# Two stacked transformer blocks in split fp32: the memory keys kept as high and low parts, and four raw weight buffers instead of six

## The chip, the cores and the metric

One Trainium2 chip, one core of it. The metric is the device time of one execution of the whole program, in microseconds; the kernel before took 2056.8 us (median of 3 runs, 2055.86 to 2057.23).

## The reference

Two transformer blocks on one sequence of 256 rows of width 1024, all in fp32. The first has four layers, each a mixer, a cross attention to a memory of 256 rows and a feed-forward part with a short convolution, with a layer norm behind each. The second has two layers with other mixers that attend to a second memory. What bears on the change is this:

```python
mem_k, mem_v = jnp.split(mem @ mem_w_kv, 2, axis=-1)      # once, for all four layers
...
def memory_cross_attention(x, mem_k, mem_v, w_q, w_o):    # 4 heads of 256
    q = (x @ w_q).reshape(bsz, s, X_HEADS, X_HEAD_DIM)
    sc = jnp.einsum('bshd,bmhd->bhsm', q, mem_k).astype(jnp.float32) * (X_HEAD_DIM ** -0.5)
    p = jax.nn.softmax(sc, axis=-1)
    o = jnp.einsum('bhsm,bmhd->bshd', p.astype(mem_v.dtype), mem_v).reshape(bsz, s, D_MODEL)
    return o @ w_o
...
for i in range(DEPTH):                                    # 4 layers
    y = mixer(x)                                          # window attention, recurrent, latent, window attention
    x = layer_norm(ALPHA * x + y, ln_g[i, 0], ln_b[i, 0])
    x = layer_norm(ALPHA * x + memory_cross_attention(x, mem_k, mem_v, x_w_q[i], x_w_o[i]), ...)
    x = layer_norm(ALPHA * x + conv_glu_ffn(x, ...), ...)
```

## The kernel before

The 256 rows are two tiles of 128 partitions (t = 0 and 1); the width 1024 is eight blocks of 128 (KD). X, the residual, stays in SBUF in row form. What a matmul needs in transposed form is transposed on TensorE (L262) and split into two fp32r parts: the high part is a cast on ACT, the low part a subtract on DVE (`split`, L163 and L164). Every large product of two fp32 operands is then three matmuls, high by high, high by low and low by high (`mm3`, L158 to L160).

Weights go through `wslot`. One slot is 128x1024 in fp32, 512 KB (384 KB and less in a few products): one DMA from SP's queue into a buffer of the pool `wraw` (L77), two casts of 512 columns on ACT into hi (L83), and two subtracts on DVE into lo (L86). The second subtract sets the raw buffer free. hi and lo come from a second pool of nine slots. There are 650 slots in one execution. The pools are rings: a DMA into a raw buffer waits for the subtract that read the slot which had the buffer before, and SP takes its DMAs strictly in order, so whatever stands behind a blocked one waits too. Among those are the DMAs of the layer norms' gains and biases (`gb`, 1 MB, one buffer, L404, which waits for the last L420 of the norm before).

The program is written as cooperative threads (a dense product, an attention lane, the transposes of a row tile), and the `run` loop emits them by a planned clock; after that each engine's instructions are put in order once more by a list scheduler. So a change of a pool's size also changes the order in which an engine gets its instructions. The engines run their queues in order.

The keys and values of the memory are made first, before any layer: `mem_kv_first` computes eight key blocks of 128x256 (slots 0 to 7, `mem_w_k`) and two value tiles of 128x1024 (slots 8 to 15, `mem_w_v`), and `evac` copies them from PSUM into `memkv`, in turn with ACT (L62) and DVE (L64). The constants (identity, rope tables, mask; L245 to L254) are loaded within it; the mask's staging buffer waits for the softplus of the recurrent layer's parameters on DVE (L197 to L207). Each of the four crosses then casts the whole key tile to its own kh on ACT (L630, four casts) and takes kl by four subtracts on POOL (L631). Beside these, POOL only does the power in a few one-column instructions (L396, L1082).

A layer norm (`layer_norm_post`) adds the PSUM banks to X (L412), takes statistics (L413, L415), the scale (L395 on DVE, L396 on POOL), and then X by L419 and L420, all on DVE but for L396; behind it PE transposes X (L262). In the second block `norm_first` takes the sum of squares on ACT (L1079), the scale on DVE and POOL (L1081, L1082), and the normed row on DVE (L1084).

Of the kernel before, what the change touches and what calls it, by code (L numbers as in the profile page):

```python
# [12 lines left out]
F32 = mybir.dt.float32  # L13
F32R = mybir.dt.float32r
AF = mybir.ActivationFunctionType
ALU = mybir.AluOpType
# [3 lines left out]
P = 128  # L20
NT = 2
D = 1024
KD = D // P
# [5 lines left out]

M_SWA1, M_CAUS1, M_CAUS0, M_END = 0, 256, 384, 512  # L30

CFG = dict(hm=(1, 1), pm=(2, 2), cut=2, raw=6, hl=9, tail=8, head=3, pin=())


@with_exitstack
def model_kernel(ctx: ExitStack, tc: tile.TileContext, A, out):
    nc = tc.nc
    V, S, G, T = nc.vector, nc.scalar, nc.gpsimd, nc.tensor

    const = ctx.enter_context(tc.tile_pool(name="const", bufs=1))  # L40
    wraw = ctx.enter_context(tc.tile_pool(name="wraw", bufs=CFG["raw"]))
    whl = ctx.enter_context(tc.tile_pool(name="whl", bufs=CFG["hl"]))
    act = ctx.enter_context(tc.tile_pool(name="act", bufs=1))
# [4 lines left out]
    def bank(tag="r"):  # L48
        return psum.tile([P, 512], F32, tag=tag, name="bank", bufs=4 if tag == "r" else 2)
# [4 lines left out]
    def phase(name):  # L54
        return tc.tile_pool(name=name, bufs=2, reuse_waits="tile")
# [3 lines left out]
    def evac(dst, src):  # L59
        count["ev"] += 1  # L60
        if count["ev"] % 2:
            S.copy(dst, src)  # L62
        else:
            V.tensor_copy(dst, src)  # L64

    ring = deque(maxlen=CFG["hl"])

# [3 lines left out]
    def wslot(src, pieces, held=idle):  # L71
        res, o = [], 0
        for m in pieces:
            assert len(ring) < CFG["hl"] or not ring[0]()
            ring.append(held)
            raw = wraw.tile([P, 1024], F32, tag="raw", name="raw")
            nc.sync.dma_start(raw[:, :m], src[:, o : o + m])  # L77
            hi = whl.tile([P, 1024], F32R, tag="hi", name="hi")
            lo = whl.tile([P, 1024], F32R, tag="lo", name="lo")
            step = -(-m // CFG["cut"])  # L80
            for a in range(0, m, step):
                c = slice(a, min(a + step, m))
                S.copy(hi[:, c], raw[:, c])  # L83
            for a in range(0, m, step):
                c = slice(a, min(a + step, m))
                V.tensor_tensor(lo[:, c], raw[:, c], hi[:, c], ALU.subtract)  # L86
            res.append((hi, lo))
            o += m
        return res
# [6 lines left out]
    def pe(ins):  # L96
        if pinned[0] in CFG["pin"]:
            tc.keep_in_program_order(ins)
# [16 lines left out]
    def after(*ths):  # L115
        def f():
            if all(t is None or t.done for t in ths):
                return max([t.end for t in ths if t is not None] + [0.0])
            return None

        return f
# [34 lines left out]
    def mm3(ps, ah, al, bh, bl, first, last):  # L156
        clk[0] += 3 * (ps.shape[-1] / 2.4 + 13.5)
        pe(T.matmul(ps, ah, bh, start=first, stop=False))  # L158
        pe(T.matmul(ps, ah, bl, start=False, stop=False))  # L159
        pe(T.matmul(ps, al, bh, start=False, stop=last))  # L160

    def split(hi, lo, src):
        S.copy(hi, src)  # L163
        V.tensor_tensor(lo, src, hi, ALU.subtract)  # L164
# [14 lines left out]
        return wide(tag + "h", F32R), wide(tag + "l", F32R)  # L179

    cur = {}
    memkv = act.tile([P, 4, D], F32, tag="mkv", name="memkv")

    readers = {"x": [], "o": []}
    rows_of = [None, None]
# [27 lines left out]
    head = []  # L213
    with phase("init") as ph:
# [7 lines left out]
        for h in range(4):  # L222
            if h == 1:
                head = wslot(A["mem_w_k"][0], [1024, 1024])
            c = slice(2 * h, 2 * h + 2)
# [4 lines left out]
    def load_x():  # L230
        nc.sync.dma_start(X, A["x"])
        with phase("initx") as ph:
            xT = fresh("x")
            for h in range(4):
                c = slice(2 * h, 2 * h + 2)
                stage = ph.tile([P, 2, NT * P], F32, tag="stage", name="stage")
                nc.sync.dma_start(stage, A["xT"][:, c])
                split(xT[0][:, c], xT[1][:, c], stage)
# [5 lines left out]
    def load_constants():  # L244
        nc.sync.dma_start(ident, A["c_ident"])  # L245
        S.copy(identr, ident)
        nc.sync.dma_start(rope, A["c_rope"])
        with phase("initm") as ph:
            mst = ph.tile([P, M_END], F32, tag="mst", name="mst")
            nc.sync.dma_start(mst, A["c_mask"])  # L250
            S.copy(maskh, mst)
            sst = ph.tile([P, 2, 12], F32, tag="sst", name="sst")
            nc.sync.dma_start(sst, A["c_sel"])
            S.copy(sel, sst)  # L254
# [11 lines left out]
    def transpose_split(blocks, dst, t):  # L266
        def put(i, n, ps):
            split(dst[0][:, i : i + n, tile_cols(t)], dst[1][:, i : i + n, tile_cols(t)], ps)

        transposed(blocks, put)  # L270
# [16 lines left out]
    def col_blocks(x, n=KD):  # L287
        return [x[:, i * P : (i + 1) * P] for i in range(n)]
# [80 lines left out]
    def load_rows(w, n, per):  # L369
        return Rows(w, n, per)  # L370
# [3 lines left out]
    def project_full(src, w, post):  # L374
        project(src, load_rows(w, D, 1), HALVES, post)
# [9 lines left out]
    def rows_ready():  # L385
        return [after(r) for r in rows_of]

    def by_block(w):
        for s in range(w.shape[0]):
            for hi, lo in wslot(w[s], [1024, 1024]):  # L390
                yield hi.rearrange("p (k c) -> p k c", c=P), lo.rearrange("p (k c) -> p k c", c=P)
# [207 lines left out]
    def fed(*ths):  # L599
        return lambda: 0.0 if all(t.fed for t in ths) else None  # L600
# [4 lines left out]
    def mem_kv_first():  # L605
        first = [[x.rearrange("p (k c) -> p k c", c=P) for x in b] for b in head]
        for c, (hi, lo) in enumerate(chain(first, by_block(A["mem_w_k"][1:]))):
            ps = bank()
            for k in range(KD):
                mm3(ps[:, :256], hi[:, k], lo[:, k], cur["o"][0][:, k], cur["o"][1][:, k], k == 0, k == KD - 1)  # L610
            evac(memkv[:, c // 4, (c % 4) * 256 : (c % 4 + 1) * 256], ps[:, :256])
            if c == 5:
                load_constants()

        def post(t, ps):
            for h in range(2):
                evac(memkv[:, 2 + t, h * 512 : (h + 1) * 512], ps[h])
            if t == 0:
                load_x()

        project_full(cur["o"], A["mem_w_v"], post)

    def cross(i, post):
        pinned[0] = "s"
        with phase(f"x{i}") as ph:
            kT = memkv[:, 0:2].rearrange("p a (c n) -> p (a c) n", n=256)
            kh = ph.tile([P, KD, 256], F32R, tag="kh", name="kh", bufs=1)
            kl = ph.tile([P, KD, 256], F32R, tag="kl", name="kl", bufs=1)
            for c in range(0, KD, 2):
                S.copy(kh[:, c : c + 2], kT[:, c : c + 2])  # L630
                G.tensor_tensor(kl[:, c : c + 2], kT[:, c : c + 2], kh[:, c : c + 2], ALU.subtract)  # L631

            tq, at = {}, []
            lane = Lane(1, 3, old_read)

            def qpost(t, ps):
                q = ph.tile([P, D], F32, tag="q", name="q", bufs=1)
                for h in range(2):
                    S.mul(q[:, h * 512 : (h + 1) * 512], ps[h], 1.0 / 16)
                soon = clk[0] + 1500  # L640
                yield lambda: soon if t == 0 or lane.recs[0].scored is not None else None
                qh = ph.tile([P, KD, P], F32R, tag="qh", name="qh", bufs=1)
                ql = ph.tile([P, KD, P], F32R, tag="ql", name="ql", bufs=1)
                transpose_split(col_blocks(q), (qh, ql), 0)
                tq[t] = qh, ql

            def score_of(t):
                def score(h):
                    qh, ql = tq[t]
                    return [  # L650
                        (l[:, k], r[:, k])
                        for k in range(2 * h, 2 * h + 2)
                        for l, r in ((qh, kh), (ql, kh), (qh, kl))
                    ]

                return score

            ws, ready = load_rows(A["x_w_q"][i], D, 1), rows_ready()
            q = [dense("x", ws, HALVES, t, qpost, need=ready[t], lag=1700) for t in range(NT)]
            for t in range(NT):  # L660
                at.append(attend(
                    lane, ph, t, 4, 256, 256, score_of(t), lambda h, kt: memkv[:, 2 + kt, h * 256 : (h + 1) * 256],
                    need=lambda h0: after(q[t]), hold=fed(q[t]), cost=720,
                ))
            out_proj(A["x_w_o"][i], post, *at)
            run(*at[0], *at[1])
# [778 lines left out]
```

## Time and profile before

| what | us |
|---|---|
| runs of the kernel before, median of 3 | 2056.8 (2055.86 to 2057.23) |
| profiled execution, its own time | 2056.11 |
| span of its trace | 2054.3 |
| TensorE (PE) busy | 2028.4 (99%) |
| VectorE (DVE) busy | 1603.8 (78%) |
| ScalarE (ACT) busy | 1214.3 (59%) |
| GpSimd (POOL) busy | 59.6 (3%) |
| granted TensorE clock, mean | 0.999 |

The busy time of an engine is a sum over the span; it tells nothing of which of its waits are on the path that sets the end. That is read from the waits: a row "A <- B" there says that an instruction of A sat idle until B had finished. A wait of SP's queue (SPq) for a buffer is what a prefetch looks like when it is far ahead. HBM was read at 173 GB/s over the span, 354.75 MB.

### The profile page before, as it was taken

What the parts mean: (1) busy time and instruction counts of PE and PEld (TensorE: products, weight loads), DVE (VectorE), ACT (ScalarE), POOL (GpSimd) and SP (SyncE); (2) the same over time, 40 slices, a digit from 0 to 9 for tenths busy, and PEclk for the clock granted to TensorE, in tenths of its full rate; (3) what the DMA queues carried; (4) which work ended last, traced back from release to release, by engine and by line L of the source; (5) the groups of instructions that cost most, each with busy time, mean ns of one, the idle gap of its engine ahead of it and who ended that gap; (6) DMA issues with size and microseconds to landing.
All of it is one profiled execution on the core that took longest, in us unless ns stands there. A gap on an engine that the chain in (4) does not pass through costs nothing.

```text
span 2054.3 us, 35609 instructions
## 1 busy us (share of the span) xinstructions
PE 2028.4 (99%) x13290; PEld 1832.5 (89%) x13290; DVE 1603.8 (78%) x3327; ACT 1214.3 (59%) x2642; POOL 59.6 (3%) x62
## 2 busy tenths in 40 slices
PE   8999999999999999999999999999999999999998
PEld 7788999897899988889997889998988999988997
DVE  6887878789777788697789878787668877778775
ACT  6655656496565556465556556565556665557563
POOL 0010000002000001000000100000000000000000
PEclk9999999999999999999999999999999999999999
DMA  8533655536455452455544447554346555445551
GB/s 300 208 134 134 226 188 182 180 112 242 153 197 186 154 183 103 175 201 195 187 149 164 145 145 254 195 182 151 121 142 235 202 180 170 126 145 202 188 185 52
DMA packets 101407, 358.12 MB, mean 174 GB/s; under 512 B 11889, under 2 KB 13553, under 8 KB 99313
## 3 DMA queue, kind: packets, MB, share of 16 engines
q1 hardware_dynamic: 101232, 355.84, 49.6%
q8 instruction: 104, 1.70, 0.3%
q14 instruction: 71, 0.57, 0.1%
HBM read 354.75 MB, written 1.05 MB: 173 GB/s over the span
## 4 chain that ended last, share of the span: by engine, by line
PE 91%; DVE 5%; ACT 2%; DMA 1%; issue 1%; POOL 0%; SPq 0%; POOLq 0%; DVEq 0%; ACTq 0%
PE bank L158 27%; PE bank L160 27%; PE bank L159 27%; PE bank L557 3%; PE bank L262 2%; DVE lo L86 2%; PE bank L488 1%; PE bank L529 1%; PE bank L483 1%; ACT hi L83 1%; PE bank L478 1%; ACT pr L508 0%; DMA row<-in_mem 0%; DVE nm L501 0%; PE bank L1037 0%
## 5 line engine op out<-in xcount | busy, mean ns | idle before, releaser
L83 ACT CAST hi<-raw 128x512 fp32r<-128x512 f32 (+3 forms) x1300 | 745.2, 607 | 438.9 <-PE bank L159 202.6
L86 DVE TENSOR_TENSOR lo<-raw,hi 128x512 fp32r<-128x512 f32 (+3 forms) x1300 | 840.9, 671 | 182.7 <-ACT hi L83 178.0
L158 PE MATMUL bank<-xh,hi 128*128 128x256 f32 (+1 forms) x1936 | 547.9, 283 | 0.6 <-ACT ti L803 0.6
L160 PE MATMUL bank<-xh,lo 128*128 128x256 f32 (+1 forms) x1936 | 547.6, 283 | 0.0
L159 PE MATMUL bank<-xl,hi 128*128 128x256 f32 (+1 forms) x1936 | 547.5, 283 | 0.0
L158 PEld LDWEIGHTS bank<-xh,hi 128*128 128x128 f32 x1936 | 371.3, 192 | 4.1 <-ACT ti L803 0.9
L159 PEld LDWEIGHTS bank<-xl,hi 128*128 128x128 f32 x1936 | 371.3, 192 | 2.7
L160 PEld LDWEIGHTS bank<-xh,lo 128*128 128x128 f32 x1936 | 371.3, 192 | 0.4
L977 DVE SCALAR_TENSOR_TENSOR c<-bank,cw,c 128x254 f32<-128x254 f32 (+1 forms) x528 | 238.7, 477 | 31.0 <-ACT c L973 30.6
L158 PE MATMUL bank<-hi,xh 128*128 128x512 f32 (+4 forms) x688 | 249.5, 363 | 0.0
L160 PE MATMUL bank<-hi,xl 128*128 128x512 f32 (+4 forms) x688 | 242.1, 353 | 0.5 <-DVE xl L164 0.5
L159 PE MATMUL bank<-lo,xh 128*128 128x512 f32 (+4 forms) x688 | 241.8, 352 | 0.0
L158 PE MATMUL bank<-hi,gh 128*128 128x512 f32 x528 | 208.7, 395 | 0.2 <-ACT gh L163 0.2
L159 PE MATMUL bank<-lo,gh 128*128 128x512 f32 x528 | 206.5, 391 | 0.0
L160 PE MATMUL bank<-hi,gl 128*128 128x512 f32 x528 | 205.5, 390 | 0.0
L158 PE MATMUL bank<-hi,oh 128*128 128x512 f32 (+1 forms) x392 | 157.6, 404 | 0.0
L159 PE MATMUL bank<-lo,oh 128*128 128x512 f32 (+1 forms) x392 | 152.2, 389 | 0.5 <-DVE lo L86 0.5
L160 PE MATMUL bank<-hi,ol 128*128 128x512 f32 (+1 forms) x392 | 152.3, 389 | 0.0
L158 PEld LDWEIGHTS bank<-hi,xh 128*128 128x128 f32 x688 | 129.7, 188 | 16.2 <-issue 2.9
L160 PEld LDWEIGHTS bank<-hi,xl 128*128 128x128 f32 x688 | 129.4, 188 | 14.4 <-DVE xl L164 0.7
L159 PEld LDWEIGHTS bank<-lo,xh 128*128 128x128 f32 x688 | 129.8, 189 | 11.9
L973 ACT ACTIVATE c<-bank,cw 128x256 f32<-128x256 f32 x264 | 133.5, 558 | 0.2 <-PE bank L160 0.2
(270 smaller groups left out, 2495.1 us busy)
## 6 DMA issues: line engine op xcount, KB each, us to landing
raw<-in_f_w_up SPq DMA_DIRECT2D x176, 512.0 KB, 3.6
raw<-in_f_w_down SPq DMA_DIRECT2D x88, 512.0 KB, 3.5
raw<-in_m_w_up SPq DMA_DIRECT2D x88, 512.0 KB, 4.0
raw<-in_m_w_down SPq DMA_DIRECT2D x44, 512.0 KB, 3.6
raw<-in_m_w_qkv SPq DMA_DIRECT2D x48, 384.0 KB, 3.6
raw<-in_x_w_q SPq DMA_DIRECT2D x32, 512.0 KB, 3.5
raw<-in_x_w_o SPq DMA_DIRECT2D x32, 512.0 KB, 5.4
raw<-in_a_w_qkv SPq DMA_DIRECT2D x24, 512.0 KB, 6.0
```

Of the source, the lines that this page charges most:

```text
L83: S.copy(hi[:, c], raw[:, c])
L86: V.tensor_tensor(lo[:, c], raw[:, c], hi[:, c], ALU.subtract)
L158: pe(T.matmul(ps, ah, bh, start=first, stop=False))
L159: pe(T.matmul(ps, ah, bl, start=False, stop=False))
L160: pe(T.matmul(ps, al, bh, start=False, stop=last))
L262: pe(T.transpose(ps[:w, j * P : (j + 1) * P], b, ident))
L478: pe(T.matmul(banks[b], l, r, start=(j == 0), stop=False))
L483: pe(T.matmul(banks[b][:, i], l, r, start=(j == 0), stop=(j == len(pairs) - 1)))
L488: pe(T.matmul(banks[b][:, i], *pairs[j], start=False, stop=(j == count_ - 1 and i == g - 1)))
L557: pe(T.matmul(po[i * w : (i + 1) * w, tile_cols(c - c0)], value(h0 + h, kt)[:, off : off + w], pT[h, kt], start=(kt == 0), stop=(kt == nk ...
L973: S.activation(c[:, h], ps[:, h], AF.Identity, scale=cw[:, 2, b : b + 1], bias=cw[:, 3, b : b + 1])
L977: V.scalar_tensor_tensor(c[:, h, s:], ps[:, h, : 256 - s], cw[:, 2 - s, b : b + 1], c[:, h, s:], ALU.mult, ALU.add)
```

## The change

The memory keys are no longer kept in fp32 and split anew in each cross. `mem_kv_first` writes them by `split`, so a key block costs one ACT cast from PSUM and one DVE subtract that reads PSUM and the high part; the tile `memk` holds both parts and takes the place of `memkv`, 16 KB in each partition. The values get a tile of their own, `memv`, 8 KB. The crosses read `memk` directly, and kh, kl and their casts and subtracts (L630, L631) are gone. For the 8 KB, the raw weight ring gets four buffers instead of six. Lines behind L181 move down by one and, behind the removed ones, up by five (L404 becomes L405, L1084 becomes L1079).

```diff
-CFG = dict(hm=(1, 1), pm=(2, 2), cut=2, raw=6, hl=9, tail=8, head=3, pin=())
+CFG = dict(hm=(1, 1), pm=(2, 2), cut=2, raw=4, hl=9, tail=8, head=3, pin=())
...
-    memkv = act.tile([P, 4, D], F32, tag="mkv", name="memkv")
+    memk = act.tile([P, 2, KD, NT * P], F32R, tag="mkv", name="memk")
+    memv = act.tile([P, NT, D], F32, tag="mv", name="memv")
...
-            evac(memkv[:, c // 4, (c % 4) * 256 : (c % 4 + 1) * 256], ps[:, :256])
+            split(memk[:, 0, c], memk[:, 1, c], ps[:, :256])
...
-                evac(memkv[:, 2 + t, h * 512 : (h + 1) * 512], ps[h])
+                evac(memv[:, t, h * 512 : (h + 1) * 512], ps[h])
...
-            kT = memkv[:, 0:2].rearrange("p a (c n) -> p (a c) n", n=256)
-            kh = ph.tile([P, KD, 256], F32R, tag="kh", name="kh", bufs=1)
-            kl = ph.tile([P, KD, 256], F32R, tag="kl", name="kl", bufs=1)
-            for c in range(0, KD, 2):
-                S.copy(kh[:, c : c + 2], kT[:, c : c + 2])
-                G.tensor_tensor(kl[:, c : c + 2], kT[:, c : c + 2], kh[:, c : c + 2], ALU.subtract)
-
+            kh, kl = memk[:, 0], memk[:, 1]
...
-                    lane, ph, t, 4, 256, 256, score_of(t), lambda h, kt: memkv[:, 2 + kt, h * 256 : (h + 1) * 256],
+                    lane, ph, t, 4, 256, 256, score_of(t), lambda h, kt: memv[:, kt, h * 256 : (h + 1) * 256],
```

Two places where the order moves. The first is DVE's queue at the start of the cross behind the recurrent mixer: the last slot of that mixer's output product (raw_5320 before, raw_5309 now), the first two q slots of the cross (raw_5433 and raw_5447; raw_5422 and raw_5436 now), and the layer norm of tile t = 0 between them. Before:

```order
L86 TENSOR_TENSOR lo_5323<-raw_5320,hi_5322 128x512 x2
L86 TENSOR_TENSOR lo_5436<-raw_5433,hi_5435 128x512
L412 SCALAR_TENSOR_TENSOR X_80<-X_80,bank_5223 128x512
L412 SCALAR_TENSOR_TENSOR X_80<-X_80,bank_5224 128x512
L413 BN_STATS st_5337<-X_80 128x6 x2
L86 TENSOR_TENSOR lo_5436<-raw_5433,hi_5435 128x512
L415 BN_AGGR mv_5342<-st_5337 128x2
L86 TENSOR_TENSOR lo_5450<-raw_5447,hi_5449 128x512
L395 TENSOR_SCALAR rs_5344<-mv_5342 128x1
```

And now:

```order
L86 TENSOR_TENSOR lo_5312<-raw_5309,hi_5311 128x512 x2
L413 SCALAR_TENSOR_TENSOR X_80<-X_80,bank_5212 128x512
L86 TENSOR_TENSOR lo_5425<-raw_5422,hi_5424 128x512
L414 BN_STATS st_5326<-X_80 128x6
L413 SCALAR_TENSOR_TENSOR X_80<-X_80,bank_5213 128x512
L86 TENSOR_TENSOR lo_5425<-raw_5422,hi_5424 128x512
L414 BN_STATS st_5326<-X_80 128x6
L86 TENSOR_TENSOR lo_5439<-raw_5436,hi_5438 128x512
L416 BN_AGGR mv_5331<-st_5326 128x2
L86 TENSOR_TENSOR lo_5439<-raw_5436,hi_5438 128x512
L396 TENSOR_SCALAR rs_5333<-mv_5331 128x1
```

Both subtracts of the second q slot now stand ahead of the scale of the norm, where one did; the other stood behind its last L420.

The second is SP's queue a little later, at the end of the q weights of the same cross. Before:

```order
L77 DMA raw_5503<-in_x_w_q 128x1024
L77 DMA raw_5524<-in_x_w_q 128x1024
L77 DMA raw_5535<-in_x_w_q 128x1024
L77 DMA raw_5715<-in_x_w_o 128x1024
L404 DMA gb_5711<-in_ln_gb 128x2048
L77 DMA raw_5745<-in_x_w_o 128x1024
```

And now:

```order
L77 DMA raw_5492<-in_x_w_q 128x1024
L77 DMA raw_5513<-in_x_w_q 128x1024
L405 DMA gb_5700<-in_ln_gb 128x2048
L77 DMA raw_5524<-in_x_w_q 128x1024
L77 DMA raw_5704<-in_x_w_o 128x1024
L77 DMA raw_5734<-in_x_w_o 128x1024
```

The gb DMA has moved ahead of two weight slots: the last of the q weights and the first of the output weights.

## Rows read from the trace of the kernel before

**Rows 1.** Page, busy time of each engine, share of the span, instructions

```profile
PE 2028.4 (99%) x13290; PEld 1832.5 (89%) x13290; DVE 1603.8 (78%) x3327; ACT 1214.3 (59%) x2642; POOL 59.6 (3%) x62
```

**Rows 2.** Waits of PE, 0 to 60 us: total us, times, longest

```profile
PE bank L158 <- ACT hi L83: 7.1, 1, 7.1
```

**Rows 3.** Waits of PE, 100 to 2040 us

```profile
PE bank L262 <- DVE X L420: 2.6, 2, 1.8
PE bank L262 <- DVE row L1084: 1.8, 3, 1.0
...
PE bank L159 <- DVE lo L86: 0.5, 1, 0.5
```

**Rows 4.** Page, groups: count, busy us, mean ns, idle us before and its releaser

```profile
L83 ACT CAST hi<-raw 128x512 fp32r<-128x512 f32 (+3 forms) x1300 | 745.2, 607 | 438.9 <-PE bank L159 202.6
L86 DVE TENSOR_TENSOR lo<-raw,hi 128x512 fp32r<-128x512 f32 (+3 forms) x1300 | 840.9, 671 | 182.7 <-ACT hi L83 178.0
```

**Rows 5.** Waits of SP's queue, whole span

```profile
SPq L77 <- DVE lo L86: 1324.0, 522, 18.4
```

**Rows 6.** L86 alone, 200 to 300 us: ns min/median/max, first and last start

```profile
L86 DVE TENSOR_TENSOR lo<-raw,hi x74: 641/690/695, 201.5 to 299.3; 128x512 fp32r<-128x512 f32 x74
```

**Rows 7.** DMA issues, whole span: KB each, median us from issue to landing

```profile
raw<-in_f_w_up SPq DMA_DIRECT2D x176, 512.0 KB, 3.6
...
raw<-in_x_w_o SPq DMA_DIRECT2D x32, 512.0 KB, 5.4
...
gb<-in_ln_gb SPq DMA_DIRECT2D x12, 1024.0 KB, 4.9
```

**Rows 8.** Timeline of PE, 475 to 478.5 us: start, us, idle before and releaser

```profile
475.14 0.39 PE L158 MATMUL bank<-hi,oh 128*128 128x512 f32 x1
475.37 0.39 PE L159 MATMUL bank<-lo,oh 128*128 128x512 f32 x1
477.59 0.66 PE L262 MATMUL bank<-ident,X 128*128 128x128 f32 x4 [1.83 <-DVE X L420]
```

**Rows 9.** Timeline of DVE, 24 to 40 us

```profile
25.01 4.62 DVE L86 TENSOR_TENSOR lo<-raw,hi 128x512 fp32r<-128x512 f32 x7 [3.24 <-ACT hi L83]
...
34.43 3.69 DVE L86 TENSOR_TENSOR lo<-raw,hi 128x512 fp32r<-128x512 f32 x6
```

**Rows 10.** Instructions on the tiles gh and gl, ns min/median/max

```profile
L163 ACT CAST gh<-sg x132: 390/402/408, 223.7 to 2029.1; 128x256 fp32r<-128x256 f32 x132
L164 DVE TENSOR_TENSOR gl<-sg,gh x132: 406/418/427, 224.2 to 2029.6; 128x256 fp32r<-128x256 f32 x132
```

**Rows 11.** Instructions on the tile memkv, ns min/median/max

```profile
L630 ACT CAST kh<-memkv x16: 613/621/624, 122.8 to 1148.6; 128x512 fp32r<-128x512 f32 x16
L631 POOL TENSOR_TENSOR kl<-memkv,kh x16: 1282/1297/5573, 123.5 to 1151.5; 128x512 fp32r<-128x512 f32 x16
```

**Rows 12.** Timeline of POOL, 460 to 480 us

```profile
465.16 9.78 POOL L631 TENSOR_TENSOR kl<-memkv,kh 128x512 fp32r<-128x512 f32 x4 [70.11 <-ACT kh L630]
```

**Rows 13.** Timeline of DVE, 463 to 477 us

```profile
464.07 5.50 DVE L86 TENSOR_TENSOR lo<-raw,hi 128x512 fp32r<-128x512 f32 x9
...
472.16 1.62 DVE L86 TENSOR_TENSOR lo<-raw,hi 128x512 fp32r<-128x512 f32 x1
...
473.83 1.66 DVE L86 TENSOR_TENSOR lo<-raw,hi 128x512 fp32r<-128x512 f32 x1
```

**Rows 14.** Timeline of SP's queue, 483 to 496 us

```profile
487.00 0.33 SPq L404 DMA_DIRECT2D gb<-in_ln_gb  x1
```

**Rows 15.** Timeline of ACT, 1539 to 1542 us

```profile
1540.51 0.59 ACT L163 CAST xh<-bank 128x512 fp32r<-128x512 f32 x1
```

**Rows 16.** Timeline of SP's queue, 1536 to 1542 us

```profile
1537.12 0.33 SPq L77 DMA_DIRECT2D raw<-in_m_w_down  x1
```

**Rows 17.** L86 alone, 0 to 464 us and 476 us to the end

```profile
L86 DVE TENSOR_TENSOR lo<-raw,hi x284: 635/685/695, 7.1 to 462.9; 128x512 fp32r<-128x512 f32 x142
L86 DVE TENSOR_TENSOR lo<-raw,hi x1005: 347/684/696, 478.1 to 2024.4; 128x512 fp32r<-128x512 f32 x144, 128x384 fp32r<-128x384 f32 x18, 128x352 fp32r<-128x352 f32 x3, 128x268 fp32r<-128x268 f32 x2
```

## The prediction

> **What bounds the kernel now.** I read the page first: TensorE is busy 2028.4 us of a span of 2054.3, DVE 78%, ACT 59% [rows 1]. The profiled execution took 2056.11 us, 1.8 more than its span and 0.7 less than the median of the timed runs, 2056.8. Then the waits of PE. At the start it stands 7.1 us until the first weight is cast [rows 2]; from 100 us on the two largest named waits are the 2.6 us for X of L420 and the 1.8 us for the rows of L1084 (three times, 1.0 at most), and for a low part of a weight (L86) it waited 0.5 us in all [rows 3]. So PE has work in hand nearly always. A change can give back only these few waits; it can cost more, if weights begin to come late.
>
> So the next view is the feed of weights. One slot is a DMA, two casts and two subtracts; a cast takes 0.61 us and a subtract 0.67, 1300 of each [rows 4]. SP stood 1324 us waiting for a subtract to release a raw buffer [rows 5]. That looks like a starved queue and isn't one: SP runs ahead, and being blocked is its normal state. What counts is how long a landed slot lies there before its cast.
>
> **Four raw buffers in the steady part.** Between 200 and 300 us 74 subtracts ran [rows 6], so 37 slots, one in 2.70 us. With six buffers a slot has 6 x 2.70 = 16.2 us from issue to release. It needs 3.6 us to land [rows 7] and 0.61 + 2 x 0.67 = 1.95 us from the start of its first cast to the end of its second subtract, so about 10.6 us are slack. With four buffers it has 10.8 us, of which 5.2 are slack. The pool of hi and lo parts keeps its nine slots, so what PE has in hand does not shrink. Cost 0.
>
> **The start.** Here the ring is tight. Eight value slots follow each other, each six matmuls of 512 columns; such matmuls start 0.23 us apart [rows 8], so PE takes a slot in 1.38 us. DVE subtracted them and the two slots ahead of them between 25.01 and 38.12 us, twenty subtracts without a stop of which the rows show the first and the last piece [rows 9]: 1.31 us a slot, so it kept just ahead of PE, which waits for nothing there [rows 2]. With four buffers a slot's cycle is 3.6 + 1.95 = 5.55 us if it lands in the usual 3.6, and a slot is turned in 1.39 us: even with PE. If it lands in the 5.4 us of an x_w_o slot [rows 7] it is 1.84 us, and eight slots lose 3.7 us less the lead that the first four bring. SP itself is held there by the mask DMA of L250, which waits for the softplus on DVE; in the new order this stands behind two more small subtracts and ahead of one weight subtract that it followed, so it moves by a few tenths at most. I take 0 and keep 0 to +2.
>
> **Keys written as high and low parts.** Eight evacuations of 128x256 become eight casts and eight subtracts; the nearest rows are 0.40 and 0.42 us [rows 10]. Even without a credit for the copies that go, this is 3.2 us on ACT and 3.4 us on DVE, spread over 35 us in which DVE stood still for 3.24 us in one piece [rows 9]. Cost 0; what a subtract can delay behind it is inside the +2 above.
>
> **The casts and POOL subtracts of the crosses.** 16 ACT casts of 0.62 us go, 9.9 us, and 16 POOL subtracts of 1.30 us at the median [rows 11]. No wait of PE names kl or kh, so by themselves they are worth 0. But look at the one cross in which they took longer. After the recurrent mixer the four POOL subtracts took 9.78 us together [rows 12]; the slowest, 5.57 us [rows 11], falls there. In that stretch DVE ran nine L86 in 5.50 us, and then two single ones, at 472.16 and 473.83, took 1.62 and 1.66 us where others take 0.68: 0.94 + 0.98 = 1.9 us lost [rows 13]. Behind them in DVE's queue stand the mean and the scale of the layer norm (L415, L395), then L419 and L420, and for that X PE waited 1.83 us [rows 8]. Without POOL this chain ends up to 1.9 us sooner, and PE gains up to 1.83. The Trainium skill (SBUF — State Buffer, "Who interferes with whom") says that a DVE instruction with two SBUF inputs and a GpSimd one that reads SBUF exclude each other, the second standing still until the first is through. The stretched pairs agree. By that rule alone each POOL subtract could hold DVE for 1.3 us, which would be 21 us in the kernel; the trace has two such delays, and the sum keeps 1.9.
>
> The new order takes a part back: two subtracts of the slot behind now stand ahead of L396 (the old L395) where one did, + 0.6 us. So the chain is about 1.3 to 1.4 us earlier. I take -1.4, with ends 0 and -1.8. The ring costs little on the way there: a slot is released by a subtract four slots back, and those of this stretch end earlier than before too, one of them by moving from behind L420 to ahead of L396.
>
> Then the last q weight of this cross. In SP's queue the 1 MB gb DMA, which waits for the second tile's L420 (487.00 us [rows 14]), now stands ahead of the last x_w_q slot; before, it stood behind an x_w_o one. Issued 0.4 us behind gb and landing in 5.4 us, as x_w_o slots do there [rows 7], that slot arrives at 492.8, or 491.4 with the 1.4 us gained. Before, nothing waited for it. In the new PE order some eight 512-column matmuls of other slots (8 x 0.23 = 1.8 us) come ahead of its own. I take +0.5, with ends 0 and +1.8 (their cover gone).
>
> **Other stage starts.** fox: four small subtracts stand ahead of L1076 (the old L1081) where three did. dilated: the square row on ACT comes behind a cast whose raw is released later. PE waited for the rows of both already, up to 1.0 us [rows 3], so a delay shows in full: I take +0.3 and +0.5, ends 0 and +1.6 together. Elsewhere a late cast can stand on ACT ahead of the cast of a transposed row. The worst is at 1540.51 us [rows 15]: the slot cast before it had long landed; released four subtracts back, as the DMA issued at 1537.12 was [rows 16], it lands 3.6 us later at 1540.7, its two casts end at 1541.9, and the xh behind it starts 1.3 us late. Going through all slots in this way I count some twenty such places, of 0.1 to 1.3 us, 12 us in sum. PE shows no wait at them now, so each has some cover whose size no row gives; +0.4 for all, ends 0 and +6 (half of the 12).
>
> Sum: 0 + 0 - 1.4 + 0.5 + 0.3 + 0.5 + 0.4 = +0.3: 2056.4 against the profiled 2056.11, and with its 0.7 below the median 2057.1 us.
>
> **Rivals.** (a) Starvation, slower. In a ring of four a slot can be asked for only four subtracts ahead. At a stage's start ACT, in order, stands at a cast whose raw has not landed, the transposed rows queue behind it, and PE runs dry. Place: the twenty stage starts; price 6 to 8 us (half to two thirds of the 12), 2063 to 2065. It decides once more than a third of those delays reach PE. For it: at the start the ring is only even with PE. Against it: 5.2 us of slack in the feed-forward parts, and PE's 0.5 us for L86 today. The Trainium skill (Perfetto Trace Analysis, "Optimization Strategy") reads a gap that keeps coming back on the engine that should be full as a sign of too few buffers. PE has no such gap in this trace, and by that rule one would come here.
> (b) The two stretched subtracts are not POOL's doing, and the gb DMA costs its full +1.8: with the other +1.2 that is 2059.8. For it: nine L86 ran at full speed while POOL stood at its first. Against it: of all other subtracts none takes over 0.70 us [rows 17].
> (c) Faster: all the waits of rows 3 go, 2.6 + 1.8 + 0.5 = 4.9 us, because ACT and POOL have less to do and nothing is late: 2051.9. Against it: only 1.83 of them lie beside a POOL subtract.
>
> **How the numbers follow.** Chances: forecast 0.57, (a) 0.22, (b) 0.15, (c) 0.06. Within 0.2% (4.1 us, about what a measurement here can tell from no change) lie the forecast and (b), 0.72; slower is (a), 0.22; faster (c), 0.06. The range goes from 2054, where all of the gain comes and almost nothing is lost, to 2063.5, the near part of (a); some 0.19 is left outside.
>
> **What would show it.** Right: no L86 above 0.75 us in the cross after the recurrent mixer, and the 1.83 us wait of PE for X under 0.6; SP still blocked by L86 nearly always; PE's waits for hi and lo after the start below 2 us together; POOL at some 35 us busy. Wrong: waits of PE for hi or xh of several us, or the same wait at stage after stage; a gap on PE between 25 and 55 us; a long wait in that cross for its last q slot.

## The result and the profile after

The changed kernel took 2069.56 us (median of 4 runs, 2068.58 to 2070.78), beside 2057.02 us for the kernel before: 1.0064 times as long, interval 1.0051 to 1.0076. That is 12.5 us slower, where no change was forecast (2057.1, range 2054 to 2063.5). Its profiled execution took 2068.58 us with a span of 2066.8.

The page's busy times, as in [rows 1]:

```profile
PE 2029.2 (98%) x13290; PEld 1832.1 (89%) x13290; DVE 1603.7 (78%) x3331; ACT 1207.4 (58%) x2630; POOL 34.8 (2%) x46
```

No engine has more to do. POOL lost its 24.8 us and ACT 6.9; TensorE has the same 13290 matmuls and 0.8 us more of busy time. So nearly all of the 12.5 us of span are idle time of PE. Its waits over the whole span (us in total, times, longest), largest first, to compare with [rows 2, 3]:

```profile
PE bank L158 <- ACT hi L83: 7.4, 1, 7.4
PE bank L1032 <- DVE row L64: 3.9, 4, 1.3
PE bank L158 <- ACT gh L163: 2.8, 2, 1.4
PE bank L263 <- ACT kr L678: 2.0, 2, 1.8
PE bank L263 <- DVE row L1079: 1.9, 3, 1.2
PE bank L558 <- ACT pT L62: 1.6, 3, 1.1
PE bank L530 <- DVE ol L164: 1.4, 1, 1.4
...
PE bank L263 <- DVE X L421: 1.1, 1, 1.1
...
PE bank L159 <- DVE lo L86: 0.7, 2, 0.5
```

Look at what is not there. PE does not wait for weights: the low part of a weight costs 0.7 us in all, where it cost 0.5 [rows 3]. What is new or has grown are the waits for a hidden row (L1032, once in the feed-forward part of each of the four layers, where PE transposes it), gh, kr, pT and ol, each a result of ACT or DVE. And SP's queue tells nothing, as before [rows 5]:

```profile
SPq L77 <- DVE lo L86: 1326.1, 517, 18.4
```

The view that shows the change is the waits of ACT. Before, its casts waited for a weight DMA 14.8 us in 17 waits, and these are the three largest lines:

```profile
ACT hi L83 <- DMA raw<-in_mem_w_k: 6.1, 4, 4.2
ACT hi L83 <- DMA raw<-in_a_w_qkv: 4.4, 5, 1.8
ACT hi L83 <- DMA raw<-in_x_w_q: 3.5, 4, 1.5
```

Now it is 77.4 us in 86 waits, spread over 20 weight tensors, of which the largest three are:

```profile
ACT hi L83 <- DMA raw<-in_x_w_q: 16.4, 12, 5.0
ACT hi L83 <- DMA raw<-in_f_w_down: 9.4, 6, 2.4
ACT hi L83 <- DMA raw<-in_m_w_up: 9.1, 8, 1.7
```

How an ACT wait becomes a PE wait is seen in the first feed-forward part of the second block. ACT's timeline of the changed kernel (start, us, idle before it and its releaser; lines that are not needed left out):

```profile
1572.69 0.62 ACT L83 CAST hi<-raw 128x512 fp32r<-128x512 f32 x1 [1.69 <-DMA raw<-in_m_w_up]
1573.21 1.93 ACT L968 ACTIVATE c<-bank,cw 128x256 f32<-128x256 f32 x4
...
1577.81 0.91 ACT L976 ACTIVATE sg<-c 128x256 f32<-128x256 f32 x2
...
1579.17 0.74 ACT L163 CAST gh<-sg 128x256 fp32r<-128x256 f32 x2
```

The same instructions in the kernel before:

```profile
1561.80 0.62 ACT L83 CAST hi<-raw 128x512 fp32r<-128x512 f32 x1
1562.33 1.93 ACT L973 ACTIVATE c<-bank,cw 128x256 f32<-128x256 f32 x4
...
1567.45 0.72 ACT L981 ACTIVATE sg<-c 128x256 f32<-128x256 f32 x2
...
1568.60 0.71 ACT L163 CAST gh<-sg 128x256 fp32r<-128x256 f32 x2
```

And PE of the changed kernel:

```profile
1579.63 0.50 PE L158 MATMUL bank<-hi,gh 128*128 128x512 f32 x1 [1.38 <-ACT gh L163]
```

From the cast to gh it is 6.8 us before and 6.5 now; the chain did not get longer, it began late. The cast at 1572.69 stood 1.69 us at a DMA that had not landed. No wait of PE names the weight of that cast. But the convolution of the first hidden block (L968) stands behind it in ACT's queue, and behind that the gate and gh, for which PE then waits 1.38 us.

The largest of the new rows, L1032, comes about in the same way. This is the feed-forward part of the fourth layer in the changed kernel:

```profile
1245.71 1.14 ACT L83 CAST hi<-raw 128x512 fp32r<-128x512 f32 x2 [1.53 <-DMA raw<-in_f_w_down]
...
1246.36 1.29 DVE L86 TENSOR_TENSOR lo<-raw,hi 128x512 fp32r<-128x512 f32 x2 [1.37 <-ACT hi L83]
...
1250.05 0.42 DVE L64 COPY row<-bank 128x256 f32<-128x256 f32 x1
...
1250.52 0.55 PE L1032 MATMUL bank<-ident,row 128*128 128x128 f32 x3 [1.29 <-DVE row L64]
```

The cast stands 1.53 us at its DMA, the subtracts wait for the cast, and the copy of the row stands behind the subtracts in DVE's queue. In the kernel before PE does not wait at this place.

The start is the largest single place. ACT of the changed kernel:

```profile
40.98 1.14 ACT L83 CAST hi<-raw 128x512 fp32r<-128x512 f32 x2 [2.81 <-DMA raw<-in_mem_w_v]
44.63 1.33 ACT L163 CAST xh<-stage 128x512 fp32r<-128x512 f32 x2 [2.52 <-DMA stage<-in_xT]
...
57.28 1.14 ACT L83 CAST hi<-raw 128x512 fp32r<-128x512 f32 x2 [1.57 <-DMA raw<-in_a_w_qkv]
```

And PE a little later:

```profile
65.32 0.66 PE L263 MATMUL bank<-ident,kr 128*128 128x128 f32 x4 [1.79 <-ACT kr L678]
```

The last value slot, the staging of x and the first qkv slots come one behind the other out of SP's queue, each held by a buffer; what PE misses in the end is kr, behind the qkv casts.

In the cross behind the recurrent mixer the subtracts are no longer stretched. All L86 between 464 and 500 us of the changed kernel (ns min/median/max; [rows 13] had 1.62 and 1.66 us there):

```profile
L86 DVE TENSOR_TENSOR lo<-raw,hi x28: 636/684/693, 463.5 to 499.7; 128x512 fp32r<-128x512 f32 x28
```

But ACT stands at two q slots there and the transposed row comes late behind three casts, so PE pays at the next step (ACT, then PE):

```profile
478.15 1.14 ACT L83 CAST hi<-raw 128x512 fp32r<-128x512 f32 x2 [2.57 <-DMA raw<-in_x_w_q]
...
481.05 1.14 ACT L83 CAST hi<-raw 128x512 fp32r<-128x512 f32 x2 [0.44 <-PE bank L263]
482.09 0.58 ACT L163 CAST xh<-bank 128x512 fp32r<-128x512 f32 x1
```

```profile
482.72 0.50 PE L158 MATMUL bank<-hi,xh 128*128 128x512 f32 x1 [1.00 <-ACT xh L163]
...
489.75 1.32 PE L263 MATMUL bank<-ident,X 128*128 128x128 f32 x8 [1.06 <-DVE X L421]
```

Where the time was lost, over the whole span: both kernels start 13290 matmuls, nearly in the same order, so the start of the k-th can be compared (medians over the 60 matmuls from each time on, by the times of the kernel before).

| at, us of before | 57 | 215 | 472 | 492 | 560 | 797 | 1081 | 1240 | 1433 | 1519 | 1567 | 1738 | 1828 | 1880 |
|---|---|---|---|---|---|---|---|---|---|---|---|---|---|---|
| later by, us | 2.8 | 3.8 | 3.0 | 4.1 | 5.2 | 6.9 | 6.4 | 7.8 | 7.2 | 8.1 | 10.6 | 10.5 | 11.6 | 13.1 |

It is not one place: the start, and then a step of 0.4 to 2.5 us at most stage starts.

### The profile page after: what moved, and what is told of

It is laid out like the page before. It is cut to its first block, busy times and chain, and to the rows that moved or that the text cites. A ratio compares the mean times of both kernels' runs of the same rounds, so it can differ in the third digit from the quotient of the medians.

```text
span 2066.8 us, 35589 instructions
## 1 busy us (share of the span) xinstructions
PE 2029.2 (98%) x13290; PEld 1832.1 (89%) x13290; DVE 1603.7 (78%) x3331; ACT 1207.4 (58%) x2630; POOL 34.8 (2%) x46
## 4 chain that ended last, share of the span: by engine, by line
PE 84%; DVE 6%; DMA 5%; ACT 3%; issue 1%; POOL 0%; SPq 0%; DVEq 0%; POOLq 0%; ACTq 0%
PE bank L158 25%; PE bank L160 25%; PE bank L159 25%; PE bank L558 3%; DVE lo L86 2%; PE bank L263 2%; PE bank L530 1%; ACT hi L83 1%; PE bank L484 1%; PE bank L489 1%; DMA raw<-in_m_w_up 1%; DMA stage<-in_xT 1%; DMA raw<-in_mem_w_k 1%; ACT pr L509 1%; DMA raw<-in_x_w_q 1%
## 5 line engine op out<-in xcount | busy, mean ns | idle before, releaser
L86 DVE TENSOR_TENSOR lo<-raw,hi 128x512 fp32r<-128x512 f32 (+3 forms) x1300 | 841.8, 670 | 201.8 <-ACT hi L83 196.5
L159 PEld LDWEIGHTS bank<-lo,xh 128*128 128x128 f32 x688 | 129.9, 189 | 12.5 <-DVE lo L86 0.6
L968 ACT ACTIVATE c<-bank,cw 128x256 f32<-128x256 f32 x264 | 133.2, 558 | 0.2 <-PE bank L160 0.2
```

Source lines behind the costliest of these rows:

```text
L968: S.activation(c[:, h], ps[:, h], AF.Identity, scale=cw[:, 2, b : b + 1], bias=cw[:, 3, b : b + 1])
```

## The experiments

Theory 1: the shorter ring makes weight slots land late, at the start and at stage starts; ACT and DVE stand at them in order, and what PE needs is queued behind. Theory 2: the new splits of the keys cost the time. Theory 3: it is the new order of the instructions that the change brought with it. Ratios are to the kernel before, run beside it on the same chip, with their 95% intervals.

| run | median us | ratio | interval |
|---|---|---|---|
| ring of four alone | 2073.34 | 1.0078 | 1.0063 to 1.0093 |
| ring of five alone | 2058.01 | 1.0004 | 0.9995 to 1.0013 |
| keys split, ring of six | 2055.97 | 0.9996 | 0.9986 to 1.0005 |
| eight half buffers | 2067.52 | 1.0042 | 1.0028 to 1.0057 |
| ring of six in the order made for four | 2054.70 | 0.9987 | 0.9978 to 0.9997 |
| the same, once more | 2055.16 | 0.9992 | 0.9984 to 1.0001 |
| ring of four, then six | 2064.10 | 1.0034 | 1.0021 to 1.0047 |
| ring of four, half the bytes | 2056.16 | 0.9999 | 0.9989 to 1.0008 |
| keys split, ring of six, eight ready slots | 2056.57 | 1.0002 | 0.9992 to 1.0011 |
| the same in the order made for four | 2055.43 | 0.9995 | 0.9986 to 1.0003 |
| ring of six in the order made for three | 2052.92 | 0.9983 | 0.9974 to 0.9992 |
| keys split, ring of six, eight ready slots, order made for three | 2053.22 | 0.9985 | 0.9976 to 0.9994 |

### Each part alone

The kernel before with a ring of four:

```diff
-CFG = dict(hm=(1, 1), pm=(2, 2), cut=2, raw=6, hl=9, tail=8, head=3, pin=())
+CFG = dict(hm=(1, 1), pm=(2, 2), cut=2, raw=4, hl=9, tail=8, head=3, pin=())
```

> The kernel before with four raw buffers and nothing else changed. Theory 1 (the shorter ring makes weights land late, whatever the keys do): 2066 to 2071, 10 to 14 us above the kernel before; the two stretched subtracts in the cross after the recurrent mixer stay, so perhaps 1 us more than the changed kernel has. Theory 2 (the splits of the keys at the start and the other order of work that they bring cost the time): within 2 us of the kernel before, 2055 to 2059.

The same with `raw=5`:

> The kernel before with five raw buffers. Theory 1: part of the loss, 2058 to 2063, because a fifth buffer gives back about 2.7 us of the 5.4 us of slack in the steady part and more than half of the late landings at stage starts. Theory 2: 2055 to 2059. If the loss has a threshold at four buffers, this one is within 1 us of the kernel before.

And the changed kernel with `raw=6`; it leaves out the values' tile, copies the values to a scratch tile and reads the high parts of the keys in their place:

```diff
-CFG = dict(hm=(1, 1), pm=(2, 2), cut=2, raw=4, hl=9, tail=8, head=3, pin=())
+CFG = dict(hm=(1, 1), pm=(2, 2), cut=2, raw=6, hl=9, tail=8, head=3, pin=())
...
-    memv = act.tile([P, NT, D], F32, tag="mv", name="memv")
...
-                evac(memv[:, t, h * 512 : (h + 1) * 512], ps[h])
+                sink = ph.tile([P, 512], F32, tag="sink", name="sink")
+                evac(sink, ps[h])
...
```

> The changed kernel with six raw buffers. The values of the memory have no tile here (there is no room for it): their product is computed and copied to a scratch tile, and the crosses read the high parts of the keys as values, at the same sizes. Theory 1: 2054.5 to 2057, the loss gone and up to 1.8 us won at the cross after the recurrent mixer, where the POOL subtracts are gone. Theory 2: the loss stays, 2060 or more, with 2 us or more of it before 60 us.

The ring alone makes all of the loss (1.0078, its interval overlaps that of the whole change; 2073.3 us is more than the 2066 to 2071 expected), and the keys with six buffers none of it. Theory 2 is out. With five buffers there is no loss that can be told from none, so the price is not the same for each buffer taken away: for the sixth nothing that can be told, for the fifth all of it. ACT's waits for weight DMAs, added up over their lines, are 14.8 us with six buffers, 47.2 with five and 82.5 with four: of the first 32 us that are added the span shows 1.9 us, of the next 35 it shows 11.3 (spans of 2054.3, 2056.2 and 2067.5 us). With the keys split and six buffers PE's wait for X is down from 2.6 us in two waits [rows 3] to

```profile
PE bank L262 <- DVE X L420: 1.1, 1, 1.1
```

while with five buffers and the POOL subtracts still there it is

```profile
PE bank L262 <- DVE X L420: 2.7, 2, 1.8
```

So the 1.83 us wait went with POOL's subtracts, as the prediction had it. That the stretch hangs on them is shown: each of the six traces with POOL's subtracts has L86 of 1.5 us and more in this cross, and in the eight without them none takes over 0.70 us. That the wait hangs on the stretch is less sure: in the order made for three (below) four L86 are stretched, and the 1.83 us wait is gone all the same. In the median this is worth 0.9 us, which the interval does not tell from nothing.

### Order or depth

The order of every engine's instructions in the ring of four was taken as a table (places in the program, packed) and imposed on the kernel before, with its six buffers, by edges between neighbours that set the order and make no engine wait for another:

```diff
...
     with tile.TileContext(nc) as tc:
         model_kernel(tc, A, out)
+        impose(tc)
```

> The kernel before, with its six raw buffers, but with every engine's instructions in the order that they have in the run with the ring of four alone (the order is imposed by edges that make no engine wait for another). Theory 1 (depth: the buffers come free too late): 2055 to 2059, the loss gone although the order is that of the slow kernel. Theory 3 (the new order of instructions costs the time): 2066 to 2074. In between, both have a share.

2054.7 us where the ring of four alone took 2073.3: in its order, which the two traces show to be the same on every engine, the six buffers lose nothing, and gain a little. Theory 3 is out; what costs is the depth in the same order. (The reverse, the old order with four buffers, is not among the runs.) The gain was tried again:

> The same kernel as the one with six raw buffers in the order of the ring of four, once more beside the kernel before. If that order is a little better in itself: 2054 to 2055.5, ratio 0.9985 to 0.9995. If the first comparison was chance: 2056 to 2057.5.

0.9992, at the edge. Then with an order made for still fewer buffers:

> The kernel before with six raw buffers in the order made for a ring of three. If an order that expects late weights is better in itself, because the casts of transposed rows stand ahead of more weight casts: 2053 to 2056. If the gain of the other order was that of one or two places: 2055 to 2062.

0.9983, 3.6 us faster than the kernel before: the best of all. Its waits of PE show what the other order changes; the row of L1084 cost 1.8 us in three waits [rows 3]:

```profile
PE bank L159 <- DVE lo L86: 3.6, 5, 1.4
PE bank L262 <- DVE X L420: 1.1, 1, 1.1
PE bank L262 <- DVE row L1084: 0.9, 3, 0.4
```

It pays 3.1 us more for low parts and gets back more elsewhere, most of it from about 1050 us on by the starts of the matmuls; which of its moves do it is open.

### Depth in place and in time

Four buffers up to the last cross, six behind it:

```diff
...
+            pool = wraw if len(more) == 0 or turn6[0] % 6 < 4 else more[0]
+            turn6[0] += 1
...
-            raw = wraw.tile([P, 1024], F32, tag="raw", name="raw")
+            raw = pool.tile([P, 1024], F32, tag="raw", name="raw")
...
+            mvp.close()
+            more.append(ctx.enter_context(tc.tile_pool(name="wraw2", bufs=2)))
```

> The changed kernel with four raw buffers up to the last cross attention and six behind it (the values' tile is given up there). Theory 1: the loss up to the last cross stays (some 6.5 us by the two traces) and the rest, some 6 us, is gone: 2062 to 2065. If the loss does not belong to the stage in which the ring is short: 2056 to 2059 or 2068 and more.

2064.1, + 7.4 us, and behind 1220 us the view shows no wait of ACT for a weight DMA any more, where the changed kernel has 28 us of them. The loss sits where the ring is short.

Half the bytes in each weight DMA. The kernel leaves out the second half of each slot, and its casts and subtracts read the first half twice:

```diff
-            nc.sync.dma_start(raw[:, :m], src[:, o : o + m])
+            nc.sync.dma_start(raw[:, : m // 2], src[:, o : o + m // 2])
...
-                S.copy(hi[:, c], raw[:, c])
+                S.copy(hi[:, c], raw[:, : c.stop - c.start])
-                V.tensor_tensor(lo[:, c], raw[:, c], hi[:, c], ALU.subtract)
+                V.tensor_tensor(lo[:, c], raw[:, : c.stop - c.start], hi[:, c], ALU.subtract)
```

> The changed kernel, in which each weight DMA brings only the first half of its slot's columns, and the casts and subtracts of the second half read the first half again: the same instructions on ACT, DVE and PE, half the bytes. Theory 1, with the time from a buffer's release to the landing of its next slot as the cause: 2057 to 2062. If it is the count of buffers as such (the order that SP and the engines take, whatever a DMA takes): 2067 and more.

2056.16, less than the 2057 to 2062 expected: with four buffers and as many DMAs, casts and subtracts, the loss is gone when a DMA lands sooner. About 1 us of that is the first weight coming earlier at the start. The landings (KB, median us) with half the bytes:

```profile
raw<-in_m_w_up SPq DMA_DIRECT2D x88, 256.0 KB, 3.0
raw<-in_x_w_q SPq DMA_DIRECT2D x32, 256.0 KB, 2.6
```

and in the changed kernel:

```profile
raw<-in_m_w_up SPq DMA_DIRECT2D x88, 512.0 KB, 4.0
raw<-in_x_w_q SPq DMA_DIRECT2D x32, 512.0 KB, 4.2
```

So the loss goes with 1.0 to 1.6 us of landing. That the landing is all of it this run does not show by itself, because the order moves too when the DMAs are smaller: by name and shape ACT has another instruction than the changed kernel at 204 of 2630 places and DVE at 331 of 3331, about as many as the ring of four moves in the kernel before (200 and 299). ACT still stands 54.9 us at weight DMAs here, more than with five buffers, and PE loses nothing by it: the sum of ACT's waits is a sign and no measure.

An estimate of where the ring gets tight: with landing L and 1.95 us of casts and subtracts, a ring of n turns a slot in (L + 1.95) / n. For the 4.2 us of a q slot that is 1.54 us with four buffers and 1.23 with five; for 2.6 us it is 1.14 with four. In the first pass of a product PE takes a slot of six matmuls of 512 columns in 1.38 us. Of these three the one that loses is above 1.38. But it is no sharp rule: the eight half buffers (below) come to (3.3 + 1.95) / 4 = 1.31 us by the 3.3 us of their q halves, and lose; the value slots of the kernel before land in 7.0 us and come to (7.0 + 1.95) / 6 = 1.49, and PE waits for none of them.

Eight buffers of half the size:

```diff
-CFG = dict(hm=(1, 1), pm=(2, 2), cut=2, raw=4, hl=9, tail=8, head=3, pin=())
+CFG = dict(hm=(1, 1), pm=(2, 2), cut=2, raw=8, hl=9, tail=8, head=3, pin=())
...
-            raw = wraw.tile([P, 1024], F32, tag="raw", name="raw")
-            nc.sync.dma_start(raw[:, :m], src[:, o : o + m])
...
+            raws = [wraw.tile([P, 512], F32, tag="raw", name="raw") for c in cs]
+            for c, raw in zip(cs, raws):
+                nc.sync.dma_start(raw[:, : c.stop - c.start], src[:, o + c.start : o + c.stop])
...
```

> The changed kernel with eight raw buffers of 512 columns instead of four of 1024: the same bytes of SBUF, each half with its own DMA of 256 KB, and released by its own subtract. Theory 1, in the form that late release and late landing of whole slots make the loss: 2059 to 2065, since a half is released one subtract (0.7 us) earlier and its first cast need not wait for the second half. If only the bytes in flight count: 2068 to 2071. If twice as many DMAs cost more than they bring: above 2071.

1.0042: by the ratio a third of the loss comes back. The median, 2067.52, lies between the two ranges expected (2059 to 2065 and 2068 to 2071) and in neither. The runs spread from 2061.8 to 2067.6, and the profiled one is the longest. In its trace PE's waits are 6.0 us more than in the kernel before (24.2 instead of 18.2), and PE's busy time is 5.5 us more; why that grew is open.

### Other ways to pay for the 8 KB

Eight instead of nine ready slots (hi and lo are 8 KB a slot) pay for two raw buffers:

```diff
-CFG = dict(hm=(1, 1), pm=(2, 2), cut=2, raw=4, hl=9, tail=8, head=3, pin=())
+CFG = dict(hm=(1, 1), pm=(2, 2), cut=2, raw=6, hl=8, tail=8, head=3, pin=())
```

> The changed kernel with six raw buffers, and eight instead of nine slots of hi and lo, which pays for them. Theory 1: 2055 to 2058, since weights stand ready 7 us and more ahead of their use in most places, and one slot less is 2.7 us. If the ready slots are as tight as the raw ones: 2062 or more.

2056.57, no loss: the ready slots had 8 KB to spare, the raw ring had not. With the orders made for four and for three raw buffers and eight ready slots:

> The keys kept as high and low parts, six raw buffers and eight ready slots, in the order made for four raw buffers and eight ready slots. If both small gains add (POOL's subtracts gone, 0.9 us measured with six buffers, and the order, 2 us): 2052.5 to 2055. If the missing ready slot takes them back: 2055 to 2058.

> The changed kernel with six raw buffers and eight ready slots, in the order made for three raw buffers and eight ready slots. If the order's gain (3.6 us in the kernel before) and that of the missing POOL subtracts (0.9 us with six buffers) add: 2051 to 2053.5. If, as in the order made for four, the missing ready slot takes a part back: 2053 to 2056.

2055.43 and 2053.22. The last one beats both kernels (0.9985, interval 0.9976 to 0.9994) and keeps the split keys. But it is no faster than the old keys in the order made for three, so the two small gains do not add, or the missing slot takes one back.

## Why the prediction was wrong

- **The steady part, cost 0**: right. Between 600 and 740 us, for one, the starts of the matmuls stay within 0.4 us of the lag that they had. Slack of 5 us was enough there.
- **The start, 0 with an end of +2**: wrong, + 2.8. The arithmetic stood in the text: "even with PE" at a landing of 3.6 us and 1.84 us a slot at 5.4. I took the better landing and counted only the value slots themselves. These landed in 4.8 us at the median, and in 7.0 in the kernel before; the text used neither. PE's waits at the value slots came to only 0.2 us more, and another 0.3 is the first weight, which landed later. What paid was behind them: the staging of x and the first qkv slots, each behind the one before in SP's queue.
- **The splits of the keys, 0**: right (ratio 0.9996 with six buffers).
- **POOL's subtracts, -1.4 at the cross behind the recurrent mixer**: the mechanism was right (no stretched L86, the 1.83 us wait gone with six buffers). With four buffers most of it was spent at once on an xh that stood behind late q casts (1.00 us), and from 230 to 492 us the lag grew by 0.7 us instead of falling. That "the ring costs little on the way there" was wrong: these q slots took 6.9 and 7.0 us to land, not 3.6. (In the kernel before, slots of this burst took up to 6.5 us; six buffers covered that.)
- **The gb DMA ahead of the last q slot, +0.5**: no wait of PE names that slot, though it landed at 497.5 us and not at 491.4.
- **fox and dilated, +0.3 and +0.5**: PE's wait at the fox row fell from 0.47 to 0.20 us, at the dilated one it grew from 0.95 to 1.24. Small either way.
- **Other stage starts, +0.4 with ends 0 and +6**: this is the step that failed. The list was good. The step from "PE shows no wait at them now" to +0.4 of the 12 us was not: that "each has some cover" was taken as cover enough, while its size stood in no row. A wait that isn't there says that the cover was enough for the old lateness, not how much is left. About 9 us came from these places (the lag grew from 4.1 us at 492 to 13.1 at 1880), half as much again as the end that I gave. The hidden rows of L1032 alone are 3.9 us, with the step at 215 us. It is rival (a), with its mechanism, above its price of 6 to 8 us, which left out the start; its chance of 0.22 was too low.
- **The signs to watch for**: those for "right" misled. All of them came: no L86 above 0.70 us in the cross, the 1.83 us wait gone, SP blocked by L86 as before, PE's waits for hi and lo after the start under 2 us, POOL 34.8 us busy. None of them sees the loss, since it shows as waits for what ACT and DVE make behind a late cast. Of those for "wrong" one came, the same wait at stage after stage (L1032).

That PE's waits stand behind late casts in ACT's and DVE's queues is read from the timelines at four places; at the others it is only likely. That the depth of the ring is the cause is shown by the runs with six buffers in the same order and with two more buffers behind the last cross. That it acts through the time from release to landing rests on ACT's waits for weight DMAs and on the run with half the bytes, whose order moved too; there it is likely and not shown.

## What to carry to other kernels

The depth of a prefetch ring is judged at the busiest burst, not in the steady part. A first estimate sets (landing under load + time until release) / buffers against the time in which the consumer takes one piece; here it told four full buffers from five, and failed for eight half ones, so a run with one buffer less or more is the better guide. The price need not grow evenly: one buffer less cost nothing that could be told, two cost 0.8%. Engines that work in order turn a late prefetch into waits for other things, so look at the waits of the engine that receives the DMA, not at those for the weights. If buffers must be given up, take them where pieces lie ready longest, and try the deep ring with an instruction order made for a shallow one (worth 0.17% at best here).

## What the runs showed of the hardware

- Half the bytes save 1.0 to 1.6 of some 4 us of landing, and q slots that were asked for in a burst (some 1.2 us apart) took up to 7.0 us.
- In a burst a slot landed later with a longer ring: the eight value slots at the start took 7.0 us at the median with six buffers (kernel before), 6.3 with five, 5.3 with four (ring of four alone) and 4.8 (changed kernel). So a shorter ring got back a part of what it lost.
- A DVE subtract with two operands in SBUF beside a POOL subtract took up to 1.66 us instead of 0.68, or POOL's took 5.57 instead of 1.30, and the stretch was gone with the POOL subtracts. Which of the two stood depended on DVE's queue: while nine DVE subtracts ran back to back, POOL's stood; behind a gap of 0.18 us (ring of four alone) the two took turns, three DVE subtracts in a row at 1.77 us and POOL's at 1.74.
